# A transformer kernel of two blocks: softmax probabilities scaled before their transposes, not the output after its products

## The chip, the cores and the metric

The kernel runs on one core of a Trainium2 chip. Its engines each work through an own list of instructions, in order: TensorE (PE in the profile, its weight loads PEld), VectorE (DVE), ScalarE (ACT), GpSimd (POOL) and SyncE (SP, which here issues the loads of weights). The metric is the time of one execution on the device, in microseconds (us).

## The reference

The reference runs a first block of two layers (differential attention with a convolution, then a state-space layer with latent attention) on 256 tokens of width 1024, and a second block of two layers on its output and on 256 context tokens. The change is in the attentions of the second block. Cut to these:

```python
def na_latent(q, k, v, k_ctx, v_ctx, bias, row_idx):           # "n": 8 heads of 64
    s_win = einsum(q, k[window]) * SCALE + bias                # window keys, bias and mask
    s_ctx = einsum(q, k_ctx) * SCALE                           # 256 context keys
    p = softmax(concatenate([s_win, s_ctx]))
    return p_win @ v[window] + p_ctx @ v_ctx

def gqa_latent(q, k_all, v_all):                               # "g": 8 query, 2 key heads
    return softmax(q @ k_all.T * SCALE) @ v_all                # 256 + 256 keys

# second_block, for both layers: ya = na_latent(...), yb = gqa_latent(...) of the tokens;
# in layer 0 also softmax_attn of the context tokens among themselves (256 keys), both kinds
x = x + g1 * ((sigmoid(ga) * (ya @ w_pa) + sigmoid(gb) * (yb @ w_pb)) @ w_o)
```

Everything is in float32. Softmax divides each row of exponentials by its sum, and the product with v is linear, so that 1/sum may be multiplied in before the product or after it.

## The kernel before, in words

**Queues and order.** The program is cut into steps: functions that each issue some instructions. They stand in queues by letter: `m` is the main stream, `c` the whole stream of the context tokens (its attention included), `a` the two main attentions, `x` the products of their gates, `d` the modulation vectors. A table written by hand, `ORDER` (L161), says in which order steps are taken from the queues, and so fixes each engine's list. A step can defer a part of itself: `defer(n, fn, us)` (L296) puts `fn` behind later steps, until these have brought up an estimated cost of `us`; `due` (L287) runs what is due after each step, `undefer` (L301) forces it. `LATE` (L159) holds the two delays used by the softmax, 0.6 for the maximum and 1.0 for the exponential.

**Weights.** Weights come by DMA as `raw` tiles (L327). ACT copies the high part (`uh`, L349), VectorE subtracts for the low part (`ul`, L350, some 1.2 us for 1024 columns), and each product of a weight is three products (L369 to L371). These are most of TensorE's work.

**An attention of the second block** (`attention2`, L1844). An item is one kind (g or n), one tile of 128 queries, one head; with the 256 + 256 keys of a main attention a row has 512 numbers. There are 32 items for each of the two layers, 64 in all. The context attention has 256 keys only, and an item holds two heads (n = 2); there are 16 such items, counted from 0 in the order of the program, as the main items are from 0 to 63 over both layers. A pipeline takes for each i the steps scores(i), out(i-2), trans(i-1):

- scores: products of q and k (L1861) into a bank of PSUM; for kind n VectorE adds the bias (L1867). Then, deferred, VectorE takes the maximum (L875) and its negation (L879), and later ACT the exponential (L869), which also adds up the row's sum `sm` (ACCUMULATOR rows).
- trans: four transposes on TensorE (L893) into a bank of PSUM, the copy `probT` on ACT (L895), and on VectorE the reciprocal `ri` of the sum (L886).
- out, once for a pair of heads: products of v and `probT` (L1891) into one half of the bank `psn`, 64 partitions for each head; then products of `ri`, spread over 64 columns, with the identity (L1894) into the other half, which puts 1/sum of each query in each row. ACT copies that half to `sr` (L1908, `factor`), and VectorE multiplies the first by it into `oh` (L1903, `norm`). When all four pairs of heads are there, `oh` is split into a high and a low part for the next products (L395 on ACT, L389 on VectorE).

The pools of PSUM are `d` (4 banks, products of weights), `s` (3 banks, scores and transposes) and `n` (1 bank).

Other lines that the prediction touches: L406 to L412 are a small inverse square root on VectorE, L1091 a multiplication by it and L1092 TensorE's transposes of that, in the first block; L589, L592 and L599 are one set of the residual and its split on VectorE, L594 its ACT part; L1063 is a multiplication by a scalar per row in the first block's differential attention.

Of the kernel before, what the change touches and what calls it, by code (L numbers as in the profile page):

```python
# [12 lines left out]
AF = mybir.ActivationFunctionType  # L13
ALU = mybir.AluOpType
# [3 lines left out]
P = 128  # L18
# [134 lines left out]
class Kern:  # L153
# [279 lines left out]
    def stats_b(self, y):  # L433
        n = self.ps("n")
        for j in range(2):
            self.bcast(n[:, P * j:P * (j + 1)], y, j)
        R = self.sb("work", "R", [P, T], bufs=3)
        self.nc.scalar.activation(R, n[:, :T], AF.Copy)
        return R

    def stats_steps(self, st, acc, key, dim=D, late=None):
# [3 lines left out]
        def b():  # L445
            st["R" + key] = self.stats_b(st["rs" + key])

# [33 lines left out]
    def xs(self, st):  # L481
        return lambda: [st["x"][:, k, :] for k in range(KD)]
# [59 lines left out]
    def norm_steps(self, s, key, acc, xs, kt, gain, dim):  # L542

        def begin():
# [3 lines left out]
            for k in range(kt):  # L548
                t = self.w1("nt")
                self.nc.vector.scalar_tensor_tensor(t, xs()[k], gain(k), s["R" + key], ALU.mult, ALU.mult)  # L550
                self.split(*s[key][k], t)
# [184 lines left out]

    def scaled(self, src, R):

        t = self.w2("sc", [P, 2, T])
        self.nc.vector.tensor_tensor(t, src, R[:, None, :].to_broadcast([P, 2, T]), ALU.mult)  # L740
        return t
# [107 lines left out]
        return us  # L849


    def softmax(self, ps, groups, scale, keys, d, it, pre=None, tile=None):


        nc = self.nc
        mx = self.sb("work", "mx", [P, 2], bufs=4)[:, :groups]
        nm = self.sb("work", "nm", [P, 2], bufs=4)[:, :groups]
        sm = self.sb("work", "sm", [P, 2], bufs=8)[:, :groups]
        pt = (tile or self.w2)("prob", [P, 512])[:, :groups * keys].rearrange("p (g k) -> p g k", g=groups)
        d[it] = pt, sm  # L860
        one = not isinstance(ps, list)

        key = (id(d), it)
        self.held.append((key, 1 if one else groups))

        def exp():
            self.held.remove((key, 1 if one else groups))
            for g in range(groups):
                nc.scalar.activation(pt[:, g, :], ps[:, g, :] if one else ps[g], AF.Exp, bias=nm[:, g:g + 1], scale=scale, accum_out=sm[:, g:g + 1])  # L869

        def peak():
            if pre:
                pre()
            if one:
                nc.vector.tensor_reduce(mx, ps, AX.X, ALU.max)  # L875
            else:
                for g in range(groups):
                    nc.vector.tensor_reduce(mx[:, g:g + 1], ps[g], AX.X, ALU.max)
            nc.vector.tensor_scalar(nm, mx, -scale, None, ALU.mult)  # L879
            self.defer(0, exp, self.LATE[1])  # L880

        self.defer(0, peak, self.LATE[0], key=key)
# [961 lines left out]
    def attention2(self, st, kvs, local, kinds="ng"):  # L1844


        nc = self.nc
        d = {}
        K = T * len(kvs)
        n = 512 // K  # L1850

        def scores(it):
            kind, qt, h0 = it
            ps = self.ps("s").rearrange("p (g k) -> p g k", g=n)
            for a in range(n):
                h = h0 + 2 * a
                b = slice(64 * (h % 2), 64 * (h % 2) + 64)
                q = st[kind + "q"][b, h // 2, P * qt:P * qt + P]
                for i, kv in enumerate(kvs):
                    k = kv["nk"][b, h // 2, :] if kind == "n" else kv["gk"][b, (h // 4 + h) % 2, :]  # L1860
                    nc.tensor.matmul(ps[:, a, T * i:T * i + T], lhsT=q, rhs=k, start=True, stop=True)  # L1861
            pre = None
            if kind == "n" and local:
                def pre():
                    w = st["bias"][:, 6 * h0 + 2 - 2 * qt:6 * h0 + 6 - 2 * qt, ::-1]
                    v = ps[:, 0, :T].rearrange("p (j u) -> p j u", u=64)
                    nc.vector.tensor_tensor(v, v, w, ALU.add)  # L1867
            self.softmax(ps, n, 1.0 if kind == "n" else 0.125, K, d, it, pre)

        def trans(it):  # L1870
            self.undefer((id(d), it))
            pt, sm = d[it]
            t, r = self.transpose_prob(pt.rearrange("p g k -> p (g k)"), 512), self.recip(sm)
            for a in range(n):
                d[it[0], it[1], it[2] + 2 * a] = t[:, K * a:K * a + K], r[:, a:a + 1]

        def out(it):

            kind, qt, h0 = it
            if h0 % 2 == 0:  # L1880
                return
            o = self.ps("n").rearrange("p (a g t) -> p a g t", a=2, t=P)
            nk = K // P
            for g in range(n):
                m = h0 // 2 + g
                two = [d.pop((kind, qt, 2 * m + a)) for a in range(2)]
                for i in range(nk):
                    kv, k = kvs[i // 2], i % 2
                    for a in range(2):
                        c = 64 * (2 * m + a if kind == "n" else m // 2)  # L1890
                        nc.tensor.matmul(o[64 * a:64 * a + 64, 0, g, :], lhsT=kv[kind + "v"][:, k, c:c + 64],  # L1891
                                         rhs=two[a][0][:, P * i:P * i + P], start=i == 0, stop=i == nk - 1)
                for a in range(2):
                    nc.tensor.matmul(o[64 * a:64 * a + 64, 1, g, :], lhsT=two[a][1].to_broadcast([P, 64]), rhs=self.ident,  # L1894
                                     start=True, stop=True)
            m = h0 // 2
            if m == 0:
                d[kind, qt] = self.w2("oh", [P, 4, P])
            oh = d[kind, qt]
            R = self.w1("sr")[:, :P * n].rearrange("p (g t) -> p g t", g=n)  # L1900

            def norm():
                nc.vector.tensor_tensor(oh[:, m:m + n, :], o[:, 0, :n, :], R, ALU.mult)  # L1903
                if m + n == 4:
                    self.defer(0, lambda: st["ysink"](kind, qt, d.pop((kind, qt))))

            def factor():
                nc.scalar.activation(R, o[:, 1, :n, :], AF.Copy)  # L1908
                self.defer(0, norm)

            self.defer(0, factor, key="n")

        heads = (0, 1, 4, 5) if n == 2 else range(8)
        items = [(kind, qt, h) for kind in kinds for qt in range(2) for h in heads]
        return self.pipeline(items, [(scores, 0.86, 0), (out, 0.5 * n, 2), (trans, 0.44, 1)])

    def gate_steps(self, st, l, pool=None):
# [354 lines left out]
```

## Time and profile before

| | us |
|---|---|
| median of 3 runs | 2039.46 |
| lowest, highest | 2037.99, 2041.78 |
| the profiled execution | 2035.8 |
| its span | 2034.0 |
| TensorE busy | 1927.8 (95%) |
| VectorE busy | 1361.2 (67%) |
| ScalarE busy | 988.7 (49%) |

The span runs from the first to the last instruction of the profiled execution; times in the timeline are us from its start. The mean granted clock of TensorE was 0.978 of full speed. Busy shares are averages over stages: the two main attentions stand at about 1155 to 1320 and 1620 to 1780 us, the context attention at about 170 to 330 us.

### The profile page before, as it was taken

The numbers are of one execution on the slowest core, as the hardware profiler recorded it, in microseconds if no ns is written. First come the engines' busy times: TensorE is split into PE (matmuls) and PEld (weight loads), VectorE is DVE, ScalarE is ACT, GpSimd is POOL, SyncE is SP. The second block draws the span as 40 slices with busy tenths as digits, with TensorE's granted clock in tenths as the row PEclk, the third lists the DMA queues.
The fourth block names the chain that finished last, engine by engine and source line by source line (L and its number), as shares of the span: only waits on it lengthen the run. The fifth ranks groups of instructions, "written<-read, shape, count | busy, mean of one in ns | idle before, by whom it ended". The sixth has DMA issues, their size and how long they took to land.

```text
span 2034.0 us, 38003 instructions
## 1 busy us (share of the span) xinstructions
PE 1927.8 (95%) x15646; PEld 1785.2 (88%) x15646; DVE 1361.2 (67%) x2655; ACT 988.7 (49%) x1680; POOL 71.9 (4%) x112
## 2 busy tenths in 40 slices
PE   8889999999989999989996999989999899979998
PEld 7678889999878999789996888889999888879998
DVE  6997668777778678666655745676655755566554
ACT  5355665444445453554443455445444455535443
POOL 0212000000000000000001100000000100000000
PEclk9999999999989999999998999999999999999999
DMA  7756636666748665766556633345555643244553
GB/s 255 247 193 207 195 110 201 202 218 220 230 133 241 205 187 141 236 200 217 194 174 188 156 101 86 122 145 173 182 175 199 159 120 89 81 149 158 179 177 109
DMA packets 383775, 353.51 MB, mean 174 GB/s; under 512 B 14705, under 2 KB 370545, under 8 KB 383089
## 3 DMA queue, kind: packets, MB, share of 16 engines
q1 hardware_dynamic: 378336, 333.77, 51.9%
q0 software_dynamic: 4688, 15.73, 3.3%
q8 instruction: 123, 2.02, 0.4%
q10 hardware_dynamic: 576, 1.57, 0.2%
q14 instruction: 52, 0.42, 0.1%
HBM read 344.36 MB, written 6.68 MB: 173 GB/s over the span
## 4 chain that ended last, share of the span: by engine, by line
PE 76%; DVE 14%; ACT 4%; DMA 4%; issue 2%; SPq 0%; ACTq 0%; DVEq 0%
PE psd L369 21%; PE psd L371 20%; PE psd L370 20%; DVE ul L350 4%; PE pss L1861 4%; ACT uh L349 3%; PE pss L893 2%; PE psn L1891 2%; DMA raw<-in_w_in 2%; DVE cy L999 1%; PE psd L1657 1%; DMA raw<-in_l_w_in 1%; DMA raw<-in_w_mod 1%; PE psd L827 1%; DVE xres L592 1%
## 5 line engine op out<-in xcount | busy, mean ns | idle before, releaser
L350 DVE TENSOR_TENSOR ul<-raw,uh 128x1024 fp32r<-128x1024 f32 (+3 forms) x556 | 657.5, 1190 | 365.3 <-ACT uh L349 363.3
L349 ACT ACTIVATE uh<-raw 128x1024 fp32r<-128x1024 f32 (+3 forms) x556 | 566.0, 1025 | 337.1 <-PE psd L370 272.3
L369 PE MATMUL psd<-xacth,uh 128*128 128x256 f32 x2192 | 633.9, 289 | 9.9 <-ACT grp L703 3.1
L371 PE MATMUL psd<-xacth,ul 128*128 128x256 f32 x2192 | 626.2, 286 | 5.1 <-DVE ul L350 5.1
L370 PE MATMUL psd<-xactl,uh 128*128 128x256 f32 x2192 | 626.2, 286 | 0.6 <-DVE xactl L599 0.5
L369 PEld LDWEIGHTS psd<-xacth,uh 128*128 128x128 f32 x2192 | 425.8, 194 | 28.2 <-issue 13.4
L371 PEld LDWEIGHTS psd<-xacth,ul 128*128 128x128 f32 x2192 | 425.9, 194 | 6.6 <-DVE ul L350 6.5
L370 PEld LDWEIGHTS psd<-xactl,uh 128*128 128x128 f32 x2192 | 426.0, 194 | 1.9 <-DVE xactl L599 1.0
L369 PE MATMUL psd<-slot,uh 128*128 128x256 f32 x896 | 256.0, 286 | 0.5 <-ACT uh L349 0.5
L371 PE MATMUL psd<-slot,ul 128*128 128x256 f32 x896 | 251.4, 281 | 2.6 <-DVE ul L350 2.6
L370 PE MATMUL psd<-slot,uh 128*128 128x256 f32 x896 | 251.0, 280 | 0.0
L371 PE MATMUL psd<-hh,ul 128*128 128x256 f32 x704 | 198.1, 281 | 0.6 <-DVE ul L350 0.3
L369 PE MATMUL psd<-hh,uh 128*128 128x256 f32 x704 | 198.0, 281 | 0.0
L370 PE MATMUL psd<-hl,uh 128*128 128x256 f32 x704 | 197.5, 280 | 0.0
L369 PEld LDWEIGHTS psd<-slot,uh 128*128 128x128 f32 x896 | 169.6, 189 | 7.4 <-issue 5.2
L371 PEld LDWEIGHTS psd<-slot,ul 128*128 128x128 f32 x896 | 169.3, 189 | 3.3 <-DVE ul L350 3.3
L370 PEld LDWEIGHTS psd<-slot,uh 128*128 128x128 f32 x896 | 169.4, 189 | 0.0
L371 PEld LDWEIGHTS psd<-hh,ul 128*128 128x128 f32 x704 | 132.0, 188 | 1.6 <-DVE ul L350 1.6
L369 PEld LDWEIGHTS psd<-hh,uh 128*128 128x128 f32 x704 | 132.5, 188 | 0.4 <-issue 0.4
L370 PEld LDWEIGHTS psd<-hl,uh 128*128 128x128 f32 x704 | 132.5, 188 | 0.0
L869 ACT ACTIVATE prob<-pss,nm 128x512 f32<-128x512 f32 (+2 forms) x124 | 70.2, 568 | 22.3 <-DVE nm L879 18.9
L875 DVE TENSOR_REDUCE mx<-pss 128x1 f32<-128x512 f32 (+1 forms) x80 | 55.2, 689 | 34.4 <-PE pss L1861 33.2
(480 smaller groups left out, 2528.4 us busy)
## 6 DMA issues: line engine op xcount, KB each, us to landing
raw<-in_w_mod SPq DMA_DIRECT2D x48, 1024.0 KB, 5.5
raw<-in_w_ffn_in SPq DMA_DIRECT2D x40, 1024.0 KB, 5.1
raw<-in_w_in SPq DMA_DIRECT2D x32, 1024.0 KB, 5.7
raw<-in_w_ffn_in SPq DMA_DIRECT2D x52, 512.0 KB, 5.2
raw<-in_w_in SPq DMA_DIRECT2D x48, 512.0 KB, 5.2
raw<-in_w_ffn_out SPq DMA_DIRECT2D x24, 1024.0 KB, 4.9
raw<-in_l_w_gate SPq DMA_DIRECT2D x20, 1024.0 KB, 5.3
raw<-in_l_w_up SPq DMA_DIRECT2D x20, 1024.0 KB, 5.3
```

Of the source, the lines that this page charges most:

```text
L349: self.nc.scalar.activation(q.h, src, AF.Copy)
L350: self.nc.vector.tensor_tensor(q.l, src, q.h.bitcast(F32), ALU.subtract)
L369: mm(ps, lhsT=wh, rhs=ah, start=start, stop=False)
L370: mm(ps, lhsT=wh, rhs=al, start=False, stop=False)
L371: mm(ps, lhsT=wl, rhs=ah, start=False, stop=stop)
L592: nc.vector.tensor_tensor(x(m), x(m), d.pop(m), ALU.add)
L827: mm(d[i][j], lhsT=ah[:, s], rhs=u.h[:, k, :], start=kk == 0, stop=False)
L869: nc.scalar.activation(pt[:, g, :], ps[:, g, :] if one else ps[g], AF.Exp, bias=nm[:, g:g + 1], scale=scale, accum_out=sm[:, g:g + 1])
L875: nc.vector.tensor_reduce(mx, ps, AX.X, ALU.max)
L893: self.nc.tensor.transpose(t[:, k * P:(k + 1) * P], w[:, k * P:(k + 1) * P], self.ident)
L1861: nc.tensor.matmul(ps[:, a, T * i:T * i + T], lhsT=q, rhs=k, start=True, stop=True)
L1891: nc.tensor.matmul(o[64 * a:64 * a + 64, 0, g, :], lhsT=kv[kind + "v"][:, k, c:c + 64], rhs=two[a][0][:, P * i:P * i + P], start=i == 0, s ...
```

## The change

`softmax` gets an argument `norm`. With it, the exponential defers a new function `unit`, by 0.6 of cost: it takes the reciprocal of the sum and multiplies the probabilities by it in place, one `tensor_scalar` on VectorE per head (512 columns for a main item, two times 256 for a context item). `trans` no longer takes a reciprocal. In `out` the products of `ri` with the identity are gone; the bank has only one half in use; and the deferred part is a copy by ACT to `oh` in place of the copy `sr` and the multiplication. The first block's attentions call `softmax` without `norm` and stay as they are.

```diff
-    def softmax(self, ps, groups, scale, keys, d, it, pre=None, tile=None):
+    def softmax(self, ps, groups, scale, keys, d, it, pre=None, tile=None, norm=False):
...
             for g in range(groups):
                 nc.scalar.activation(pt[:, g, :], ps[:, g, :] if one else ps[g], AF.Exp, bias=nm[:, g:g + 1], scale=scale, accum_out=sm[:, g:g + 1])
+            if norm:
+                self.defer(0, unit, self.LATE[0])
+
+        def unit():
+            r = self.recip(sm)
+            for g in range(groups):
+                nc.vector.tensor_scalar(pt[:, g, :], pt[:, g, :], r[:, g:g + 1], None, ALU.mult)
...
-            self.softmax(ps, n, 1.0 if kind == "n" else 0.125, K, d, it, pre)
+            self.softmax(ps, n, 1.0 if kind == "n" else 0.125, K, d, it, pre, norm=True)
...
-            t, r = self.transpose_prob(pt.rearrange("p g k -> p (g k)"), 512), self.recip(sm)
+            t = self.transpose_prob(pt.rearrange("p g k -> p (g k)"), 512)
             for a in range(n):
-                d[it[0], it[1], it[2] + 2 * a] = t[:, K * a:K * a + K], r[:, a:a + 1]
+                d[it[0], it[1], it[2] + 2 * a] = t[:, K * a:K * a + K]
...
-            o = self.ps("n").rearrange("p (a g t) -> p a g t", a=2, t=P)
+            o = self.ps("n")[:, :P * n].rearrange("p (g t) -> p g t", t=P)
...
-                        nc.tensor.matmul(o[64 * a:64 * a + 64, 0, g, :], lhsT=kv[kind + "v"][:, k, c:c + 64],
-                                         rhs=two[a][0][:, P * i:P * i + P], start=i == 0, stop=i == nk - 1)
-                for a in range(2):
-                    nc.tensor.matmul(o[64 * a:64 * a + 64, 1, g, :], lhsT=two[a][1].to_broadcast([P, 64]), rhs=self.ident,
-                                     start=True, stop=True)
+                        nc.tensor.matmul(o[64 * a:64 * a + 64, g, :], lhsT=kv[kind + "v"][:, k, c:c + 64],
+                                         rhs=two[a][:, P * i:P * i + P], start=i == 0, stop=i == nk - 1)
...
-            R = self.w1("sr")[:, :P * n].rearrange("p (g t) -> p g t", g=n)
-
-            def norm():
-                nc.vector.tensor_tensor(oh[:, m:m + n, :], o[:, 0, :n, :], R, ALU.mult)
+
+            def evac():
+                nc.scalar.activation(oh[:, m:m + n, :], o, AF.Copy)
                 if m + n == 4:
                     self.defer(0, lambda: st["ysink"](kind, qt, d.pop((kind, qt))))
 
-            def factor():
-                nc.scalar.activation(R, o[:, 1, :n, :], AF.Copy)
-                self.defer(0, norm)
-
-            self.defer(0, factor, key="n")
+            self.defer(0, evac, key="n")
```

TensorE's list loses its rows of L1894, and nothing else in it changes its place. VectorE's list shows where the new work stands. After the change line numbers are 7 higher from the softmax on: L882 is the maximum, L886 the negation, L893 the reciprocal, L1874 the bias, and L876 the new multiplication. First VectorE around main item 16, before; `sm_14793` is its sum, and each row is line, operation, output, inputs and size:

```order
L1867 TENSOR_TENSOR pss_14788<-pss_14788,bias_13507 128x256
L875 TENSOR_REDUCE mx_14791<-pss_14788 128x1
L879 TENSOR_SCALAR nm_14792<-mx_14791 128x1
L886 RECIPROCAL ri_14804<-sm_14730 128x1
L1867 TENSOR_TENSOR pss_14807<-pss_14807,bias_13507 128x256
L875 TENSOR_REDUCE mx_14810<-pss_14807 128x1
L879 TENSOR_SCALAR nm_14811<-mx_14810 128x1
L886 RECIPROCAL ri_14837<-sm_14793 128x1
L1903 TENSOR_TENSOR oh_14579<-psn_14818,sr_14829 128x128
```

The same place after the change, where `sm_14767` is the sum of item 16 and `prob_14768` its probabilities:

```order
L1874 TENSOR_TENSOR pss_14762<-pss_14762,bias_13491 128x256
L882 TENSOR_REDUCE mx_14765<-pss_14762 128x1
L886 TENSOR_SCALAR nm_14766<-mx_14765 128x1
L1874 TENSOR_TENSOR pss_14779<-pss_14779,bias_13491 128x256
L882 TENSOR_REDUCE mx_14782<-pss_14779 128x1
L886 TENSOR_SCALAR nm_14783<-mx_14782 128x1
L893 RECIPROCAL ri_14800<-sm_14767 128x1
L876 TENSOR_SCALAR prob_14768<-prob_14768,ri_14800 128x512
L389 TENSOR_TENSOR xyg_14516<-oh_14555,xyg_14516 128x4x128
```

The reciprocal of item 16 stands where it stood, behind the bias, maximum and negation of item 17; the multiplication comes behind it, and the transposes of item 16 now need it. L1903 is gone from the rows.

Second, VectorE at items 6 and 7 of the context attention (`mx_3031` and `mx_3057` are their maxima), before:

```order
L875 TENSOR_REDUCE mx_3031<-pss_3028 128x2
L879 TENSOR_SCALAR nm_3032<-mx_3031 128x2
L886 RECIPROCAL ri_3051<-sm_2924 128x2
L875 TENSOR_REDUCE mx_3057<-pss_3054 128x2
L879 TENSOR_SCALAR nm_3058<-mx_3057 128x2
L1668 TENSOR_REDUCE mod_73_381<-psn_3063 128x4
L1670 TENSOR_TENSOR mod_73_381<-mod_73_381,vecs_64 128x4
L406 TENSOR_SCALAR rs_v_3097<-ssq_2332 128x4
```

And after (L1675 and L1677 are the lines 1668 and 1670 of before):

```order
L882 TENSOR_REDUCE mx_3033<-pss_3030 128x2
L886 TENSOR_SCALAR nm_3034<-mx_3033 128x2
L893 RECIPROCAL ri_3061<-sm_3035 128x2
L876 TENSOR_SCALAR prob_3036<-prob_3036,ri_3061 128x256 x2
L882 TENSOR_REDUCE mx_3057<-pss_3054 128x2
L886 TENSOR_SCALAR nm_3058<-mx_3057 128x2
L1675 TENSOR_REDUCE mod_73_381<-psn_3067 128x4
L1677 TENSOR_TENSOR mod_73_381<-mod_73_381,vecs_64 128x4
L893 RECIPROCAL ri_3095<-sm_3059 128x2
L876 TENSOR_SCALAR prob_3060<-prob_3060,ri_3095 128x256 x2
L406 TENSOR_SCALAR rs_v_3100<-ssq_2338 128x4
```

Item 6's reciprocal and two multiplications now stand ahead of item 7's maximum, and item 7's ahead of L406. The lists of GpSimd and SyncE are the same as before; on ACT the copies L1908 turn into copies to `oh`, and in a few places the split L395 comes one step earlier.

## Rows read from the trace of the kernel before

**Rows 1.** The page's busy times, and its chain that ended last, by engine.

```profile
PE 1927.8 (95%) x15646; PEld 1785.2 (88%) x15646; DVE 1361.2 (67%) x2655; ACT 988.7 (49%) x1680; POOL 71.9 (4%) x112
...
PE 76%; DVE 14%; ACT 4%; DMA 4%; issue 2%; SPq 0%; ACTq 0%; DVEq 0%
```

**Rows 2.** Groups by line and form: line, engine, tiles, shapes, count | busy us, mean ns | idle.

```profile
L893 PEld LDWEIGHTS pss<-consts,prob 128*128 128x128 f32 x338 | 36.7, 141 | 17.8 <-issue 7.8 <-ACT probT L895 4.6 <-ACT prob L869 3.2
...
L1894 PE MATMUL psn<-consts,ri 128*64 128x128 f32 x192 | 20.1, 278 | 0.0
...
L886 DVE RECIPROCAL ri<-sm 128x1 f32<-128x1 f32 x76 | 11.7, 154 | 0.0
...
L1903 DVE TENSOR_TENSOR oh<-psn,sr 128x128 f32<-128x128 f32 x32 | 9.3, 290 | 41.0 <-ACT sr L1908 40.7
...
L1063 DVE TENSOR_SCALAR wt<-prob,r 128x256 f32<-128x256 f32 x4 | 1.4, 354 | 0.1
...
L1063 DVE TENSOR_SCALAR wt<-prob,r 128x128 f32<-128x128 f32 x4 | 1.1, 287 | 0.1
```

**Rows 3.** Timeline (start, length, engine, line, tiles [idle before <-releaser]), a group of L1894.

```profile
217.67 0.25 PEld L1894 LDWEIGHTS psn<-consts,ri 128*64 128x64 f32 x4
...
217.89 0.25 PEld L1891 LDWEIGHTS psn<-probT,slot 128*64 128x64 f32 x4
```

**Rows 4.** Timeline at the transposes of main item 16.

```profile
1238.33 0.42 PEld L893 LDWEIGHTS pss<-consts,prob 128*128 128x128 f32 x4 [0.17 <-issue]
...
1238.53 0.15 DVE L886 RECIPROCAL ri<-sm 128x1 f32<-128x1 f32 x1
```

**Rows 5.** Timeline at the transposes of main item 10.

```profile
1215.37 0.15 DVE L886 RECIPROCAL ri<-sm 128x1 f32<-128x1 f32 x1
...
1215.70 0.42 PEld L893 LDWEIGHTS pss<-consts,prob 128*128 128x128 f32 x4 [0.17 <-issue]
```

**Rows 6.** Timeline at the transposes of main item 11.

```profile
1219.85 0.15 DVE L886 RECIPROCAL ri<-sm 128x1 f32<-128x1 f32 x1
...
1220.21 0.25 PEld L893 LDWEIGHTS pss<-consts,prob 128*128 128x128 f32 x2
```

**Rows 7.** Timeline at the transposes of main item 27.

```profile
1283.48 0.42 PEld L893 LDWEIGHTS pss<-consts,prob 128*128 128x128 f32 x4 [0.76 <-ACT prob L869]
...
1284.43 0.15 DVE L886 RECIPROCAL ri<-sm 128x1 f32<-128x1 f32 x1
```

**Rows 8.** Timeline at the transposes of main item 32.

```profile
1632.54 1.22 DVE L350 TENSOR_TENSOR ul<-raw,uh 128x1024 fp32r<-128x1024 f32 x1
...
1632.75 0.42 PEld L893 LDWEIGHTS pss<-consts,prob 128*128 128x128 f32 x4 [0.64 <-ACT prob L869]
```

**Rows 9.** Timeline at the transposes of the first context item.

```profile
187.11 0.20 PEld L893 LDWEIGHTS pss<-consts,prob 128*128 128x128 f32 x2 [0.26 <-ACT prob L869]
```

**Rows 10.** Timeline at context items 6 and 7.

```profile
246.71 0.69 DVE L875 TENSOR_REDUCE mx<-pss 128x2 f32<-128x512 f32 x1 [0.15 <-PE pss L1861]
...
247.35 0.20 ACT L869 ACTIVATION_READ_ACCUMULATOR prob<-pss,nm 128x1 f32 x1
...
247.80 0.16 DVE L406 TENSOR_SCALAR rs_v<-ssq 128x4 f32<-128x4 f32 x1
...
248.00 0.17 DVE L407 TENSOR_SCALAR rs_y<-rs_v 128x4 int32<-128x4 int32 x1
...
248.40 0.47 ACT L869 ACTIVATE prob<-pss,nm 128x256 f32<-128x256 f32 x1
...
250.31 0.73 PEld L1092 LDWEIGHTS pss<-consts,ot 128*128 128x128 f32 x4 [0.94 <-DVE ot L1091]
```

**Rows 11.** Timeline at context item 11.

```profile
290.48 0.42 DVE L1903 TENSOR_TENSOR oh<-psn,sr 128x256 f32<-128x256 f32 x1 [1.01 <-ACT sr L1908]
...
293.84 0.73 PEld L1861 LDWEIGHTS pss<-slot,slot 64*128 64x128 f32 x4 [1.83 <-ACT probT L895]
...
295.00 0.47 DVE L599 SCALAR_TENSOR_TENSOR xactl<-xres,vecs,xacth 128x256 fp32r<-128x256 f32 x1
```

## The prediction

> **What bounds the kernel now.** I read first the page's shares, then its chain of waits, then groups by line, then the timeline around the attentions. TensorE is busy 95% of the span and holds 76% of the chain that ended last, VectorE 14% [rows 1]. TensorE takes its instructions in order. So a delay of one of them is lost unless a later wait of TensorE shrinks, and a product taken away gives back only the time by which the next one can start earlier. The change takes products away, and it puts work of VectorE between an exponential and the transposes of its result. Two sums have to be set against each other.
>
> **What goes.** 48 groups of four products L1894 go: 192 rows, 20.1 us busy [rows 2]. That is not what they cost. In the timeline the four weight loads of a group start at 217.67 and the next load, of L1891, at 217.89 [rows 3]: 0.22 us a group, 48 x 0.22 = 10.6 us at most. The other bound is the whole busy time, 20.1 us or 0.42 a group, as if nothing else ran beside it. I take 0.22, which is read where a group ends and the next work begins.
>
> The Trainium skill, "TensorE: Matmul & The Clock Gate", section "Part 3: Packing small matmuls — row/col tiling", says that products in different column groups of the array run at once, and that a pack takes one product's time and some 4 ns for each further one; so a removed pair frees one product's time and not two, which speaks against the change. The trace agrees (0.22 us for two pairs); by the busy time instead, the sum below would be 7 us lower (35 x 0.20).
>
> The multiplication L1903 also goes, and ACT's copy of the factor, L1908, becomes a copy of the product, of the same shape: 0 on ACT. I put the loss of L1903 itself at 0: nothing on TensorE waits for it at once, the next products that need its result being whole steps away. If that cover were gone, it would be a gain of 0.29 us [rows 2] in each place. But VectorE stood idle 41 us ahead of these multiplications, waiting for the copy [rows 2], and held back what was queued behind; that is in a rival below.
>
> **What comes.** A reciprocal of 128x1 takes 154 ns, a multiplication by a per-row scalar 287 ns for 128 columns and 354 for 256 [rows 2]: 67 ns for 128 more, so 0.49 us for 512, bounded by 0.354 (the half-size row) and 0.71 (twice it). Dependent instructions on VectorE stand 0.04 us apart (L406 ends at 247.96, L407 starts at 248.00 [rows 10]), which I also take for the hand-off to TensorE. From the start of the reciprocal to the transposes that is 0.15 + 0.04 + 0.49 + 0.04, about 0.73 us where VectorE is free. VectorE gets 64 x 0.49 + 32 x 0.354 = 42.7 us more and loses some 12, beside 67% [rows 1].
>
> What matters is which transposes have less than that left, and what stands ahead of the multiplication. The order after the change puts it behind the next item's bias, maximum and negation, or behind a weight split L350. I went through all 64 items of the two main attentions: from the start that the reciprocal can have at its new place, plus 0.73, against the start of the transposes' weight load. For 45 items a gate or token product of TensorE stands in between and covers it: nothing; without that cover each would lose what the next four do. The other 19:
> - six behind the next item's bias and maximum. Item 16: reciprocal at 1238.53 at the earliest, transposes at 1239.27 in place of 1238.33 [rows 4]: +0.94. The six: 0.94, 0.94, 0.87, 0.86, 0.93, 0.85 = 5.4.
> - three without a bias. Item 10: 1215.37 + 0.73 = 1216.10 for 1215.70 [rows 5]: 0.40 each, 1.2.
> - eight behind a split. Item 11: 1219.85 + 0.74 = 1220.59 for 1220.21 [rows 6]: 0.38. The eight: 0.53, 0.38, 0.89, 0.88, 0.38, 0.38, 0.38, 0.40 = 4.2.
> - four whose transposes wait for the exponential already, so have no slack. Item 27: they waited 0.76 and started at 1283.48; the multiplication stands behind the next maximum, 1284.43 + 0.73 = 1285.16 [rows 7]: +1.68. Item 32: behind a split that starts at 1632.54 and takes 1.22: 1633.76 + 0.65 (the reciprocal overlaps its end) = 1634.41 for 1632.75 [rows 8]: +1.66. The other two: 1.66 and 0.65. Together 5.65.
>
> Main attentions: 16.5. They add up, because the next scores, copies, exponentials and splits all follow the delayed transposes in their engines' orders.
>
> Context attention (16 items, two heads each, two multiplications of 256 columns):
> - The first item's transposes already wait for their exponential (the second pair starts at 187.11 after 0.26 [rows 9]): a reciprocal and two multiplications, 0.9, less what their overlap saves: +0.8.
> - Items 6 and 7: item 6's exponential ends at 247.55, and its multiplications now stand ahead of item 7's maximum, which ran at 246.71. That maximum comes at about 248.35, item 7's exponentials (two of 0.47 and their sums) end near 250.3, and its own multiplications stand ahead of the chain that begins with L406: 251.07 in place of 247.80. For the end of that chain TensorE's transposes L1092 had already waited 0.94, until 250.31 [rows 10]: +3.3.
> - Item 11: its multiplications stand behind five sets of L589, L592, L599, whose last ended at 295.47, or some 1.35 earlier once L1903 (290.48, after a wait of 1.01) doesn't hold them up. The transposes then end near 295.8, the copy 0.6 later, and the scores that waited 1.83 and started at 293.84 come at about 296.1 [rows 11]: +2.3.
>
> Context: 6.4. A removed group inside a chain that is now late gives nothing back: 13 of 48 (9 main, 4 context). Credit kept: 35 x 0.22 = 7.7.
>
> **The sum.** 16.5 + 6.4 - 7.7 = +15.2 on the profiled execution's 2035.8: 2051.0. The median of the runs, 2039.5, lies 3.7 above that execution, so the forecast for the median is 2054 (2054.7, fraction dropped). Its own range is 2047 to 2062: the credit by the busy time makes it 7 lower, a multiplication of 0.71 in place of 0.49 some 5 higher (22 places), and the rest is for places that I misjudged.
>
> **Rivals.**
> - Partly absorbed. The transposes' weight loads lost 7.8 us to issue time [rows 2], 0.17 us at a time, and a longer wait hides such a gap; and what stood behind L1903 comes sooner. Two gaps of 0.17 hidden at each of 22 places make 7.5: 2054 - 7.5 = 2046.5. Against it: a load that another engine releases pays its own hand-off.
> - No change: the credit is whole, 10.6, and half of the waits are paid back by later waits that shrink, leaving 11.5 of 22.9: 2039.5 + 0.9 = 2040.4. For it: TensorE still idles 5% of the span, some of it behind the attentions. Against it: at 95% busy [rows 1] little is left to shrink, and what is left waits for engines that are delayed with it.
> - The other side, faster: without L1903 holding it, VectorE reaches every multiplication in time except where the transposes wait for their exponential already, in five places (four main, one context). Each grows by 0.54 (a multiplication of 0.354) to 0.73, 2.7 to 3.7, against the whole 10.6: 2032 to 2033. It decides from a mean wait under 0.48 us at the 22 places (10.6 / 22); my mean is 22.9 / 22 = 1.04. For it: those 41 us [rows 2]. Against it: in the order the next maximum or a split stands ahead of the multiplication, and these end by TensorE's scores and ACT's split, not by L1903.
> - VectorE bounds the context attention: its work there lies between chains of the other streams, and more of the 16 items push such a chain as 6, 7 and 11 do. At 2.1 us a piece (6.4 / 3) for half of the 16 that is 17 in place of 6.4: 2065; for all, 2082.
>
> That the products go and the multiplications come is plain in the order of the instructions, so "it doesn't do what it says" is no rival.
>
> **Chances.** Forecast (2047 to 2062) 0.60; partly absorbed 0.13; no change 0.10; faster 0.09; VectorE bounds 0.08. A difference of 0.2%, 4.1 us, is about what can be told from none: 2035.4 to 2043.5 counts as the same. So faster 0.09, same 0.10, slower 0.81. The range that holds 8 in 10 leaves out the faster case and most of no change below, and the upper part of the last above: 2041 to 2066.
>
> **What would show it.** The waits of the transposes' weight loads then name the new multiplication, in some 19 of the 64 main items and for 0.4 to 1.7 us; a multiplication of 512 columns lasts about 0.49; the transposes L1092 at 250.31 come some 3 us later; TensorE's busy time hardly falls. I am wrong if those waits are short, if a removed group frees 0.4 us or more, or if TensorE's other waits shrink by what the transposes lose.

## The result: slower, and by more than the waits

The changed kernel took 2073.6 us in the median of 4 runs (2070.4 to 2078.4), against 2039.2 before: a ratio of 1.0169 (95% interval 1.0145 to 1.0193), 34 us more. The direction was as forecast, the size was not: the range ended at 2066. Its profiled execution took 2070.4 us. The page's rows that answer to [rows 1]:

```profile
PE 1932.6 (93%) x15454; PEld 1786.2 (86%) x15454; DVE 1391.9 (67%) x2711; ACT 989.4 (48%) x1680; POOL 72.5 (4%) x112
...
PE 73%; DVE 16%; ACT 4%; DMA 4%; issue 2%; SPq 0%; ACTq 0%; DVEq 0%
```

TensorE is busy 5 us more than before, although 20 us of products L1894 are gone, and VectorE has moved from 14% to 16% of the chain. The new multiplications in the groups by form (after the change: L876 multiplication, L893 reciprocal, L900 transposes, L1099 for L1092):

```profile
L876 DVE TENSOR_SCALAR prob<-prob,ri 128x512 f32<-128x512 f32 x64 | 31.1, 487 | 2.3
...
L876 DVE TENSOR_SCALAR prob<-prob,ri 128x256 f32<-128x256 f32 x32 | 9.9, 350 | 0.6
```

0.487 and 0.350 us: the estimates of 0.49 and 0.354 hold. The transposes in the same view, before (L893) and after (L900); the last part is TensorE's idle time ahead of them and what ended it:

```profile
L893 PE MATMUL pss<-consts,prob 128*128 128x128 f32 x338 | 55.4, 283 | 1.3 <-ACT prob L869 1.2
...
L900 PE MATMUL pss<-consts,prob 128*128 128x128 f32 x338 | 56.7, 289 | 23.7 <-DVE prob L876 22.6 <-DVE ri L893 0.9
```

They now wait 22.6 us for the multiplication. The timeline at main items 10, 16, 27 and 32, to be read against [rows 5, 4, 7, 8] in that order, and then at item 59:

```profile
1232.99 0.15 DVE L893 RECIPROCAL ri<-sm 128x1 f32<-128x1 f32 x1
1233.18 0.49 DVE L876 TENSOR_SCALAR prob<-prob,ri 128x512 f32<-128x512 f32 x1
...
1233.78 0.42 PEld L900 LDWEIGHTS pss<-consts,prob 128*128 128x128 f32 x4 [0.84 <-PE psn L1898]
...
1256.51 0.15 DVE L893 RECIPROCAL ri<-sm 128x1 f32<-128x1 f32 x1
...
1256.69 0.49 DVE L876 TENSOR_SCALAR prob<-prob,ri 128x512 f32<-128x512 f32 x1
...
1257.30 0.42 PEld L900 LDWEIGHTS pss<-consts,prob 128*128 128x128 f32 x4 [1.38 <-issue]
...
1306.26 0.15 DVE L893 RECIPROCAL ri<-sm 128x1 f32<-128x1 f32 x1
...
1307.05 0.42 PEld L900 LDWEIGHTS pss<-consts,prob 128*128 128x128 f32 x4 [2.56 <-issue]
...
1658.76 1.22 DVE L350 TENSOR_TENSOR ul<-raw,uh 128x1024 fp32r<-128x1024 f32 x1
...
1660.69 0.55 PEld L900 LDWEIGHTS pss<-consts,prob 128*128 128x128 f32 x4 [2.35 <-issue]
...
1783.07 0.42 PEld L900 LDWEIGHTS pss<-consts,prob 128*128 128x128 f32 x4 [2.49 <-issue]
```

The pieces are the forecast ones: 0.15 for the reciprocal, 0.49 for the multiplication, then the load of the transposes. Lining up TensorE's weight loads of both traces one by one and subtracting the starts gives what each place added: item 10 0.45 (forecast 0.40), 16 0.99 (0.94), 27 1.81 (1.68), 32 1.71 (1.66). All such steps of the main attentions together make 16.4 us; forecast 16.5. The context attention, against [rows 10] and [rows 11]:

```profile
206.99 0.17 DVE L893 RECIPROCAL ri<-sm 128x2 f32<-128x2 f32 x1 [2.43 <-ACT prob L869]
...
207.72 0.16 DVE L406 TENSOR_SCALAR rs_v<-ssq 128x4 f32<-128x4 f32 x1
...
210.22 0.77 PEld L1099 LDWEIGHTS pss<-consts,ot 128*128 128x128 f32 x4 [3.96 <-DVE ot L1098]
...
257.84 0.16 DVE L406 TENSOR_SCALAR rs_v<-ssq 128x4 f32<-128x4 f32 x1
...
260.35 0.77 PEld L1099 LDWEIGHTS pss<-consts,ot 128*128 128x128 f32 x4 [3.35 <-DVE ot L1098]
...
307.85 0.47 DVE L599 SCALAR_TENSOR_TENSOR xactl<-xres,vecs,xacth 128x256 fp32r<-128x256 f32 x1
...
308.25 0.15 DVE L893 RECIPROCAL ri<-sm 128x2 f32<-128x2 f32 x1
...
308.90 0.72 PEld L900 LDWEIGHTS pss<-consts,prob 128*128 128x128 f32 x4 [5.42 <-ACT xacth L594]
```

L1099 at 260.35 is L1092 of 250.31: 3.7 us were added up to there (forecast 3.3), 1.5 of them by 256.15, at products that wait for another chain of VectorE, and 2.2 in the wait shown. The transposes of item 11 wait 5.4 us behind the last L599, a net 3.7 (forecast 2.3). And 3.1 us were added at 210.22, at the first of the two groups of L1092, where another item's multiplications also stand ahead of L406. That place was not in the forecast. With 0.85 at the first item the context's waits come to 11.4 (forecast 6.4).

Waits of 16.4 and 11.4 less the credit of 7.7 that the forecast kept are 20 us, not 34. The rest shows in the granted clock. TensorE's clock has two levels here, 2.4 GHz (1.00 in the rows) and 1.2 GHz (0.50). The windows of the changed kernel: length, busy time of PE, PEld, DVE, ACT and POOL, then the granted clock, and last the DMA's share and GB/s:

```profile
210.25:213.67 3.42, 3.42 (x16) 3.38 (x17) 1.97 (x8) 1.63 (x2) 0.00 (x0) 0.50 1.14 310
258.04:271.69 13.65, 11.33 (x40) 8.96 (x41) 8.90 (x30) 5.07 (x13) 0.00 (x0) 0.50 0.09 33
305.83:316.07 10.24, 7.13 (x27) 6.00 (x28) 9.36 (x29) 5.92 (x15) 0.86 (x2) 0.50 0.08 26
316.07:330.00 13.93, 13.93 (x113) 12.51 (x113) 9.96 (x24) 8.83 (x20) 0.00 (x0) 1.00 0.47 153
1312.76:1316.17 3.41, 3.41 (x18) 3.41 (x18) 2.83 (x6) 1.00 (x2) 0.00 (x0) 0.50 0.00 0
1660.92:1664.33 3.41, 3.41 (x18) 3.41 (x17) 1.08 (x1) 1.54 (x2) 0.00 (x0) 0.50 0.01 2
1783.80:1790.62 6.82, 6.82 (x27) 5.99 (x28) 2.99 (x6) 2.18 (x4) 0.00 (x0) 0.50 0.19 58
```

Each row at 0.50 stands at or behind a wait of the weight loads: 4.0 us until 210.22, 3.4 until 260.35, 5.4 until 308.90 (the rows of these last two begin while TensorE still waits), 2.6 until 1307.05 and 1.3 more at the next item, 2.4 until 1660.69, 2.5 until 1783.07. In the kernel before, the same stretches have one such row, 3.4 us at 286, behind a wait of 1.61:

```profile
285.17 0.71 PE L417 MATMUL psn<-consts,rs_y 128*128 128x128 f32 x4 [1.61 <-DVE mod L1668]
...
286.37:289.78 3.41, 3.41 (x27) 2.70 (x25) 3.06 (x8) 1.53 (x5) 0.00 (x0) 0.50 0.66 217
```

The length of a wait alone doesn't decide it: at 638.71 the weight loads of the changed kernel had waited 3.17 us for a DMA, and the clock stayed at 1.00:

```profile
638.71 0.37 PEld L1664 LDWEIGHTS psd<-raw,cs 128*32 128x32 f32 x12 [3.17 <-DMA raw<-in_w_mod]
...
638.00:660.00 22.00, 21.29 (x176) 18.36 (x176) 17.66 (x38) 12.94 (x26) 0.00 (x0) 1.00 0.97 257
```

What half clock costs is in the spacing of the products, first inside the second row at 0.50, then behind it:

```profile
268.11 0.41 PE L369 MATMUL psd<-xacth,uh 128*128 128x256 f32 x1
...
268.32 0.41 PE L370 MATMUL psd<-xactl,uh 128*128 128x256 f32 x1
...
268.54 0.41 PE L371 MATMUL psd<-xacth,ul 128*128 128x256 f32 x1
...
274.23 0.28 PE L371 MATMUL psd<-xacth,ul 128*128 128x256 f32 x1
...
274.35 0.28 PE L369 MATMUL psd<-xacth,uh 128*128 128x256 f32 x1
...
274.47 0.28 PE L370 MATMUL psd<-xactl,uh 128*128 128x256 f32 x1
```

0.21 us from product to product in place of 0.12. If that holds for all products there, 0.09 of each 0.21 us of TensorE's busy time is lost: in 35.5 us (the PE column of the six rows at 0.50) 15.2 us, less 1.5 for the row that was there before, so an estimate of 13.7. Then 20 + 13.7 comes to the 34 that were measured. That is an account of one pair of traces; the experiments test it.

### The profile page after: what moved, and what is told of

It reads as the page before. It is cut to its first block, busy times and chain, and to the rows that moved or that the text cites. A ratio compares the mean times of both kernels' runs of the same rounds, so it can differ in the third digit from the quotient of the medians.

```text
span 2068.6 us, 37670 instructions
## 1 busy us (share of the span) xinstructions
PE 1932.6 (93%) x15454; PEld 1786.2 (86%) x15454; DVE 1391.9 (67%) x2711; ACT 989.4 (48%) x1680; POOL 72.5 (4%) x112
## 4 chain that ended last, share of the span: by engine, by line
PE 73%; DVE 16%; ACT 4%; DMA 4%; issue 2%; SPq 0%; ACTq 0%; DVEq 0%
PE psd L369 20%; PE psd L371 20%; PE psd L370 20%; DVE ul L350 5%; PE pss L1868 4%; ACT uh L349 3%; PE pss L900 2%; DMA raw<-in_w_in 2%; PE psn L1898 1%; DVE cy L1006 1%; PE psd L1664 1%; DMA raw<-in_l_w_in 1%; DVE mx L882 1%; DVE prob L876 1%; PE psn L417 1%
## 5 line engine op out<-in xcount | busy, mean ns | idle before, releaser
L369 PE MATMUL psd<-xacth,uh 128*128 128x256 f32 x2192 | 637.9, 291 | 11.4 <-ACT grp L703 4.3
L902 ACT ACTIVATE probT<-pss 128x512 f32<-128x512 f32 (+2 forms) x100 | 53.8, 542 | 58.6 <-PE pss L900 58.5
```

The source lines that it names most:

```text
L369: mm(ps, lhsT=wh, rhs=ah, start=start, stop=False)
L902: self.defer(0, lambda: self.nc.scalar.activation(o[:, :keys], t[:, :keys], AF.Copy))
```

## The experiments

Each experiment's expectation was written before it ran. Theory 1 is that account: the waits of the transposes, and behind the long ones TensorE's lower clock. Theory 2 takes the waits alone, at their forecast size; theory 3 has VectorE as the bound of the stretches. A ratio compares the times of a kernel with those of the kernel before on the same chip. "Falls behind" is the shift of TensorE's weight loads against the profiled execution before, over a stretch of it: context 150 to 330, first main attention 1150 to 1325, second 1612 to 1780 us.

| kernel | ratio (95% interval) | context | main 1 | main 2 |
|---|---|---|---|---|
| changed kernel | 1.0169 (1.0145 to 1.0193) | +15.0 | +8.8 | +9.6 |
| e1_main_only | 1.0095 (1.0061 to 1.0129) | +2.2 | +9.6 | +9.6 |
| e2_context_only | 1.0077 (1.0047 to 1.0108) | +14.5 | +1.3 | 0.0 |
| e3_no_multiply | 0.9929 (0.9905 to 0.9953) | -2.0 | -2.2 | -3.6 |
| e4_both | 1.0201 (1.0166 to 1.0235) | +16.5 | +11.9 | +10.7 |
| e5_fill | 1.0164 (1.0117 to 1.0211) | +19.0 | +7.8 | +9.0 |
| e9_fill_sized | 1.0064 (1.0039 to 1.0089) | +7.2 | +7.6 | +4.9 |
| e6_early | 1.0084 (1.0057 to 1.0111) | +14.0 | -0.3 | +1.8 |
| e7_deep | 0.9994 (0.9975 to 1.0013) | +9.8 | -5.0 | -5.7 |
| e10_deep_late | 1.0175 (1.0146 to 1.0204) | +49.7 | -3.9 | -5.7 |
| e11_before_deep_main | 0.9983 (0.9963 to 1.0003) | +1.9 | -2.4 | -2.3 |
| e8_deep_main | 0.9945 (0.9923 to 0.9968) | +1.5 | -3.8 | -5.7 |
| e12_deep_main_again | 0.9935 (0.9911 to 0.9960) | +0.2 | -4.9 | -5.8 |

Outside these stretches the shifts of one execution against another differ by several us in either direction (e1_main_only falls 7 us behind between 550 and 860), so the ratios decide and the columns say where.

**One attention at a time, and the two sides alone.** In e1 and e2 `unitary` chooses by attention whether the probabilities are multiplied or the old way is taken:

```diff
+        unitary = n == 1                  # e1_main_only; n == 2 in e2_context_only
...
-            self.softmax(ps, n, 1.0 if kind == "n" else 0.125, K, d, it, pre, norm=True)
+            self.softmax(ps, n, 1.0 if kind == "n" else 0.125, K, d, it, pre, norm=unitary)
```

> Only the two main attentions multiply their probabilities; the context attention keeps the spread 1/sum. Theory 1 (waits of the transposes plus TensorE's lower clock behind them): in the changed kernel's trace TensorE falls behind by 8.8 us over the first main attention and 9.6 over the second, 18.4 in all, so about 2039 + 18 = 2057, with the stretches at half clock beside the main attentions as in the changed kernel and those at 200 to 320 us as in the kernel before. Theory 2 (waits alone, as predicted; the rest of the 34 us is chance of the run): 2039 + 16.5 - 23 x 0.22 = 2050.

> Only the context attention multiplies its probabilities. Theory 1 (waits plus lower clock): TensorE fell behind by 15 us between 186 and 330 us of the changed kernel, so about 2054, with three stretches at half clock at about 210, 258 to 272 and 306 to 316 us. Theory 2 (waits alone, as predicted): 6.4 - 12 x 0.22 = +3.8, 2043. Theory 3 (VectorE is the bound there): longer still, 2060 and more, with VectorE busy over 90% of the stretch.

In e3 the credit stands alone (changed kernel), in e4 the cost alone (kernel before):

```diff
-            if norm:                      # e3_no_multiply, with unit() gone
-                self.defer(0, unit, self.LATE[0])
...
+            if norm:                      # e4_both; L1894, L1908 and L1903 stay
+                self.defer(0, unit, self.LATE[0])
```

> The changed kernel without its multiplication and reciprocal (the output is left without the division by the sum): what taking away L1894 and L1903 gives by itself. By the price of 0.22 us a group: 10.6 us at most, 2028 to 2031. By the busy time (0.42 a group): 2019. If L1903 on VectorE was what held the next work: below 2025. If the products were hidden: 2039.

> The kernel before with the multiplication put in and the spread products, the copy and L1903 kept (the output is divided by the sum twice): the cost by itself. Theory 1: the changed kernel's 2073.6 plus the credit that it keeps, 7.7 to 10.6: 2081 to 2084, with half-clock stretches behind the waits. Theory 2 (waits alone): 2039 + 22.9 = 2062.

Main alone costs 0.95%, 19 us (12 to 26), and context alone 0.77%, 16 us (10 to 22): together about the 34 of the whole, and both nearer to theory 1's figure (18 and 15) than to theory 2's (11 and 4). The credit alone is 14 us by the ratio (10 to 19), at or above the 10.6 of the price of 0.22, but only 7.8 by the three columns, so its size stays open. The cost alone is 41 us (34 to 48), where theory 1 says 42 to 45 and theory 2 23. With the waits as the changed kernel's trace shows them theory 2 would have 9 for e2 and 28 for e4: e4 still speaks against it, e2 hardly. Theory 3's sign is missing: in e2 VectorE is busy 69% of the window 170 to 330, and 72% in the kernel before.

**Is it the clock?** Fillers keep TensorE at work during the wait without shortening it. Each is a product of the identity with itself into the bank that the transposes overwrite (in e9; in e5 there were 26 ahead of each L1092 group, 8, 40, 16, 16, 16 elsewhere and none at item 28):

```diff
+    def fill(self, t, n):
+        for _ in range(n):
+            self.nc.tensor.matmul(t[:, :P], lhsT=self.ident, rhs=self.ident, start=True, stop=True)
...
+        self.fill(t, fill)     # by item: context 0: 5, 11: 16; main 27, 32, 59: 9, 28: 4
...
+            self.fill(t, 12 if qt else 14)     # ahead of the L1092 groups
```

> The changed kernel, with products of the identity with itself (into the bank that the next transposes overwrite) put on TensorE at seven of the longest waits: 26 ahead of each of the two L1092 groups, 8 and 40 ahead of the transposes of context items 0 and 11, 16 ahead of those of main items 27, 32 and 59. They take time that TensorE would wait, so the waits stay and only its idleness goes. If the clock's fall behind the waits costs about 12 us (theory 1), the half-clock stretches at 210, 258 to 272, 306 to 316, 1313, 1661 and 1784 us go and the time falls to 2060 to 2066. If the waits alone cost the time (theory 2), it stays at 2073 or rises by what the fillers are too long.

This one missed, and its trace says why. The timeline at the first L1092 group (here L1105):

```profile
206.62 5.88 PEld L898 LDWEIGHTS pss<-consts 128*128 128x128 f32 x52 [0.41 <-issue]
...
209.84 0.87 DVE L1104 TENSOR_SCALAR ot<-ot,rs_y 128x128 f32<-128x128 f32 x4
212.42 0.47 PEld L1105 LDWEIGHTS pss<-consts,ot 128*128 128x128 f32 x4
```

The fillers run for 5.88 us where TensorE waited 4.0, since one takes 0.226 us and not the 0.11 that I had assumed; the transposes start 2.6 us after the first L1104 begins, where in e9 below they follow it by 0.33. At item 11 forty of them ran, partly at half clock. Of the six half-clock stretches five had gone, and one of 3.4 us had come at 1769.6; the ratio was no better, as the fillers themselves made TensorE late. So it was made again with fewer:

> The filler run again with fewer products, since one takes 0.226 us and not 0.11: 14 and 12 ahead of the two L1092 groups, 5 and 16 ahead of the transposes of context items 0 and 11, 9 at main items 27, 32 and 59, 4 at 28, each less than TensorE waits there in the changed kernel. Theory 1 (the clock's fall behind the waits costs some 10 us): the half-clock stretches behind these waits go and TensorE falls behind by 10 to 12 us in the context stretch instead of 15, and by 7 to 8 in each main attention instead of 9 to 10: 2062 to 2067. Theory 2 (waits alone): as the changed kernel, 15, 9 and 10: 2073.

Both L1092 groups, the windows around them (the second held the 13.65 us at half clock), and the transposes' waits by form:

```profile
206.30 3.20 PEld L898 LDWEIGHTS pss<-consts 128*128 128x128 f32 x28 [0.41 <-issue]
...
255.83 2.42 PEld L898 LDWEIGHTS pss<-consts 128*128 128x128 f32 x21
...
258.35 0.88 DVE L1104 TENSOR_SCALAR ot<-ot,rs_y 128x128 f32<-128x128 f32 x4
258.68 0.73 PEld L1105 LDWEIGHTS pss<-consts,ot 128*128 128x128 f32 x4 [0.42 <-DVE ot L1104]
```

```profile
205.00:220.00 15.00, 14.84 (x134) 13.88 (x133) 8.76 (x26) 6.79 (x16) 1.08 (x2) 1.00 0.80 217
250.00:275.00 25.00, 23.36 (x197) 19.96 (x196) 16.45 (x50) 15.57 (x42) 0.00 (x0) 1.00 0.24 79
```

```profile
L905 PE MATMUL pss<-consts,prob 128*128 128x128 f32 x338 | 55.6, 285 | 10.1 <-DVE prob L876 9.0 <-DVE ri L893 0.9
```

The fillers end, and the transposes start when L1104 releases them, as late behind it as in the changed kernel; but the clock stays at 1.00. (The transposes' wait for L876 is 9.0 us in place of 22.6 because the fillers fill the rest.) All that is left at half clock in the three stretches is the row that the kernel before has too, now 6.8 us at 295. The time falls from 1.69% above the kernel before to 0.64%: about 21 us, more than the 7 to 12 expected, though the intervals allow 14. By the traces the three stretches lose 19.7 us in place of 33.4: 13.7 less, the same as the spacing gave. What remains is 13 us by the ratio (8 to 18) and 19.7 by the traces, where the waits as measured less the credit come to 20. That also rules theory 2 out, and theory 3: VectorE has as much work as in the changed kernel.

**What puts the multiplication late?** e6 calls `unit()` directly behind the exponential; e7 takes the transposes one item later; e10 is e7 with the context's multiplications put off until their transposes force them:

```diff
-                self.defer(0, unit, self.LATE[0])
+                unit()                                             # e6_early
...
-        return self.pipeline(items, [(scores, 0.86, 0), (out, 0.5 * n, 2), (trans, 0.44, 1)])
+        return self.pipeline(items, [(scores, 0.86, 0), (out, 0.5 * n, 3), (trans, 0.44, 2)])     # e7_deep, e10
...
+                self.defer(0, unit, self.LATE[0] if groups == 1 else 99.0)                        # e10_deep_late
```

> The changed kernel with the reciprocal and multiplication issued directly behind the exponential instead of 0.6 later: the multiplication no longer stands behind the next item's maximum at items 16, 27 and the like. If its place in VectorE's order makes the waits (theory 1), the ten such waits (about 10 us in the main attentions) shrink to about half, and with them two of the half-clock stretches: 2062 to 2068; what is late next is the next item's maximum, which now waits for the exponential. If the length of the multiplication itself is what counts: no change, 2073.

> The changed kernel with the transposes one item later (two items behind the scores, the output three). Theory 1: the waits of the transposes go, since a whole item lies between exponential and transposes; what stays is the chain of L406 and L1091 in the context stretch, whose transposes L1092 still wait some 6 us and lose clock: 2039 - 14 + 10 = 2035 (2030 to 2042). If VectorE's added 31 us bound the stretches (theory 3): 2055 and more.

> The kernel with transposes one item later in all attentions, and the context's multiplications put off until just ahead of their transposes, so that item 7's stand behind the chain of L406 and L1091 instead of ahead of it. If the multiplication's place ahead of that chain makes the loss there (theory 1), TensorE no longer falls behind by 5 us at 244 to 250 of before, and the context stretch loses 3 to 5 us instead of the 10 with the early place: 2033. If VectorE's added work itself is too much there (theory 3): 2038 or more, as before.

e6 is at 1.0084, 17 us where 23 to 29 were expected, and the main attentions come out about even: the place in VectorE's order was the cause there. The next maximum, now behind the multiplication, costs at most the 7 us by which the two columns lie above those of e3. The transposes' waits fell to this:

```profile
L900 PE MATMUL pss<-consts,prob 128*128 128x128 f32 x338 | 55.8, 286 | 9.3 <-DVE prob L876 6.8 <-DVE ri L893 2.0
```

The same row of e2 has 6.4 for L876, so nearly all that is left belongs to the context attention. The context attention gained 1 us: its multiplications stand ahead of L406 in either place, and the two L1092 groups are as late as before (3.1 and 2.2 us added). e7 came out as expected (0.9994). e10 missed by 40 us. Its transposes' row:

```profile
L900 PE MATMUL pss<-consts,prob 128*128 128x128 f32 x338 | 59.7, 300 | 32.8 <-DVE prob L876 30.6 <-ACT prob L869 1.2 <-DVE ri L893 0.8
```

Put off until the transposes ask for it, the multiplication stands behind all that VectorE has queued, and TensorE waits for that each time; 65 us of the context stretch run at half clock. The waits of the first L1092 group for L406's chain did shrink, from 4.0 to 1.5 us, but the cure cost more. None of the places tried in that stretch is good: the early ones delay a chain for which TensorE waits, the late one delays the transposes.

**The version that is faster.** The multiplication in the main attentions only, with their transposes one item later, and as a control the same shift in the kernel before:

```diff
+        unitary = n == 1
...
-        return self.pipeline(items, [(scores, 0.86, 0), (out, 0.5 * n, 2), (trans, 0.44, 1)])
+        return self.pipeline(items, [(scores, 0.86, 0), (out, 0.5 * n, 2 + unitary), (trans, 0.44, 1 + unitary)])
```

> Only the two main attentions multiply their probabilities, with the transposes one item later there; the context attention as in the kernel before. Theory 1: no wait is left and 32 of the 48 groups are gone: 2039 - 32 x 0.22 = 2032, down to 2029 with what the run without the multiplication gained above that price. Theory 3: 2045 and more.

> The kernel before with nothing but the transposes of the main attentions one item later (spread products, copy and L1903 kept): how much of the gain of the late version is due to the later transposes. By the waits for the exponential that the main attentions have (some 3 us in all): 2036 to 2038. If the gain of 9 us is the removed products, as theory 1 says for 7 of it, no more than 3 us here.

> The version with the multiplication and later transposes in the main attentions only, beside the one above on the same chip: 0.5 to 0.6% faster than the kernel before, and 4 to 7 us faster than the run above.

In e12 nothing waits for a multiplication any more:

```profile
L900 PE MATMUL pss<-consts,prob 128*128 128x128 f32 x338 | 55.5, 284 | 1.1 <-DVE ri L893 0.8 <-ACT prob L869 0.2
```

0.9945 and 0.9935: 11 and 13 us faster than the kernel before, some 46 than the changed one. The later transposes alone (e11) give 0.9983 (0.9963 to 1.0003), 3.5 us, which may be nothing; in the two columns of the main attentions they give 4.7 of the 9.5 (e8) and 10.7 (e12). So half of the gain or more is due to taking away the products and L1903, on the condition that the multiplication is not late. The median of e12 is 8.6 us below that of e11 on the same chip, more than the 4 to 7 expected.

## Why the prediction was wrong

- **What goes.** The price of 0.22 us a group, 10.6 for all, is not refuted: the credit alone measured 14 (10 to 19) by the ratio and 7.8 by the columns, 0.16 to 0.30 us a group. Removing L1903 may have added to it; the runs don't separate that. That packed products give back less than their busy time (0.42 us a group) agrees with the Trainium skill's page "TensorE: Matmul & The Clock Gate", section "Part 3: Packing small matmuls — row/col tiling".
- **What comes, main attentions.** Right in place and size: 16.4 for 16.5, in 20 places of the trace. The prediction's four groups hold 21 items, not 19, so its 22 places are 24 and its mean wait 0.95 in place of 1.04; its sum is not touched. The single figures for items 17 and 25 (0.89 and 0.88) were too high, both measured 0.44.
- **Context attention.** Half right: 11.4 for 6.4. The first L1092 group was overlooked (3.1), though it is the same chain L406 as at items 6 and 7, and item 11 came out at 3.7 for 2.3.
- **The sum.** This is the step that failed: "16.5 + 6.4 - 7.7 = +15.2". Its context term was 5 us short, and it let TensorE go on at full rate behind each wait. The runs put another 14 us (traces) to 21 us (ratios of the changed kernel and e9) there, in stretches of 3 to 14 us at half clock at and behind the waits. No rival named it, and the range took it for neither end. The trace of before had a sign, the row at half clock at 286 behind the wait of 1.61 us, and a mean granted clock of 0.978. The Trainium skill's page "TensorE: Matmul & The Clock Gate", section "Why this matters for your kernels", warns that idle gaps between products bring the clock down; the runs agree: with the waits filled, e9 has 6.8 us at half clock in these stretches in place of 41.
- **Rivals.** Waits paid back, no change and faster: none came about; the credit of e3 and the cost of e4 (-14 and +41) add up to 27, within their intervals of the 34. VectorE as a bound: 67% busy as before, and e9 is 21 us faster with the same work on it. The last rival's times, 2065 to 2082, held the measured one: in part rightly, since one more place did push the chain of L406 (3.1 us), but most of the missing time was the clock.

## What to carry to other kernels

A wait put on TensorE costs its own length, and it can cost the products behind it too, when they run at the lower clock: here 7.8 of the 15.0 us of the context stretch went when the waits were filled. Before work goes from TensorE to an engine with a queue, read what stands ahead of the new instruction in that queue at each place. In the main attentions the same multiplication cost 19 us one item ahead of its transposes (e1) and gained 11 to 13 with the transposes one item later; in all attentions it was +34 and about 0 (e7). An instruction that is put off as far as possible is not out of the way but behind everything.

## What was not expected of the hardware

- Half clock put the products of 128x256 in the rows above from 0.12 to 0.21 us apart, not to twice that.
- Fillers of no use, such as 28 weight loads (14 products) in 3.2 us of a wait in e9, kept the clock at 1.00 and made the kernel about 1% faster than without them.
